# A decoder layer on one core: the first weight loads moved to one queue, in other pieces, with one warming matmul less

## The chip, the cores and the metric

The kernel runs on one core of one Trainium2 chip. The metric is the time of one execution on the device, in microseconds (us). The core has TensorE (PE in the profile; PEld is its weight loader), VectorE (DVE), ScalarE (ACT), GpSimd (POOL) and SyncE (SP). SP and ScalarE can each issue DMA transfers on a queue of their own. Both queues are served by the same 16 DMA engines.

## The reference

One layer of a hybrid decoder on x of 256 tokens and 1024 channels. All data are float32.

```
h = rmsnorm(x, norm1_g)
u = h @ w_in                       # 1024 x 7168: x_rnn, g_rnn, q, k, v, two gates
xa = causal_dwconv(x_rnn)          # width 4
ya = rg_lru(xa) * gelu(g_rnn)
yb = moba_attention(rmsnorm(q), rmsnorm(k), v)
x = x + (sigmoid(g_a) * (ya @ w_proj_rnn) + sigmoid(g_b) * (yb @ w_proj_attn)) @ w_out
h = rmsnorm(x, norm2_g)
x = x + (gelu(causal_dwconv(h @ w_up)) * (h @ w_gate)) @ w_down
```

## The kernel before

**Products in three parts.** Every float32 operand is split into a high part, hi (a copy in the shorter format fp32r), and a remainder, lo = raw - hi. Each product is three matmuls: high by high, high by low, low by high (`mm3`, lines 301 to 304). In the profile L302, L303 and L304 are these three. The hi copy is made on ScalarE (L284, a CAST), the lo subtraction on VectorE (L285).

**The weight stream.** All weights come as a stream of 75 chunks of up to 1 MB (128 partitions by 2048 values), in the order of use. Chunks 0 to 3 are `rx`, the 1024 columns of w_in for the recurrent branch; chunks 4 to 7 are `rg`, its gate; then follow k, the blocks of the recurrent unit, q, v, the two gates, the projections, w_out, and the feed-forward weights. `load_next` issues a chunk's DMA on SP's queue, `split_part` makes its hi and lo, `advance(i)` does both up to chunk i, with loads three chunks ahead. From chunk 4 on, raw, hi and lo tiles rotate in pools of 3, 4 and 3 buffers.

**The order.** TensorE's order follows `UNITS`: rx, rg0 to rg3, k0 and so on. Each unit runs in quarters, and the table `AFTER` says which other work is given out after which quarter: `"rg0.1": "bcast"` gives out the matmul `rbcp` after the second quarter of rg0, `s5` means "split up to chunk 5", `evac0` an evacuation, and so on. A scheduler then puts each engine's instructions in order; an engine executes its queue in that order.

**The norm.** The first product works on x times the gain only (xgh and xgl, the two parts of x^T times `norm1_g`). The row factor 1/rms is applied afterwards: `norm1_stats` squares x in the tiles xs (L397), forms the factor on VectorE (L368 to L374) and two diagonal tiles `dg` (L400). `norm1_bcast` multiplies ones by dg into `rbcp` (L406) and copies it to `rbc` (L407). The evacuations of rx (`rx_evac`, L438) and rg (L680) multiply by rbc.

**The start.** The first four chunks have code of their own (lines 322 to 353 for the loads, 377 to 387 for the splits). Nine matmuls on a tile of ones (L330, `warm`) run first. Then k tiles (pieces of 256 values along each chunk's row: the 128 input channels of one step of the product) are loaded in groups: 0, then 1, then 2 and 3, 4 and 5, 6 and 7. For each group come x^T's part (L344) and one piece of each of the four chunks (L347), 128 KB each for the first two groups and 256 KB after. For k tiles 0 and 1 the pieces of chunks 2 and 3 are issued on ScalarE's queue, all the rest on SP's. `pv` (all small vectors, among them the gain) is the first transfer on ScalarE's queue, and the table load of ScalarE (L349) stands between its DMA issues. The tiles xs are loaded after the pieces of k tiles 4 and 5. `xgh` is made on ScalarE (L382), `xgl` on VectorE (L385). The rx products run k tile by k tile over the four chunks, six matmuls for each pair, 192 in all; for each output the first product needs xgh, hi of the weight piece, then xgl, then lo.

Of the kernel before, what the change touches and what calls it, by code (L numbers as in the profile page):

```python
# [1 line left out]

# [6 lines left out]
F32 = mybir.dt.float32  # L9
F32R = mybir.dt.float32r  # L10
I32 = mybir.dt.int32
AF = mybir.ActivationFunctionType
OP = mybir.AluOpType
AX = mybir.AxisListType

P = 128
S = 256
D = 1024
KT = D // P
# [8 lines left out]
V_CW, V_CB, V_BR, V_BI, V_LAM, V_QG, V_KG, V_G1, V_FW, V_FB, V_G2 = 0, 32, 40, 48, 56, 64, 65, 66, 74, 140, 162  # L28
V_N = 170

HALVES, SMALLS, WARM, RAWS = 22, 10, 9, 3
AHEAD_S, AHEAD_L = 2, 3
DVE_HI = (39, 42, 43)
KEPT = {"ups": 1, "upd": 2, "gts": 1, "gtd": 2, "u": 1, "c": 2, "ah": 3, "al": 3}
# [1 line left out]
         "gb1 gb2 gb3 pr0 pr1 pr2 pr3 pa0 pa1 pa2 pa3")  # L36
AFTER = {
    "rx0.0": "stats s4",
    "rg0.1": "bcast",
    "rg0.2": "s5 evac1",  # L40
    "rg0.3": "s6",
    "rg1.1": "evac0",
    "rg1.3": "evac3 conv0 s7",
    "rg2.0": "evac2",
    "rg2.1": "decay conv1",
    "rg3.0": "split0",
    "rg3.1": "s8",
    "k0.0": "s9",
    "k0.1": "conv2",
    "k0.2": "conv3",  # L50
    "k0.3": "split1",
    "k1.0": "s10",
    "k1.3": "s11",
    "k2.1": "s12",
    "k2.2": "s13",
    "k3.1": "s14 gelu1",
    "ri0.2": "krs",
    "ri0.3": "s15",
    "q0.1": "la0 s16 lb0",
    "q1.1": "s17",  # L60
    "q1.3": "lc0",
    "ri1.0": "s18",
    "q2.0": "ld0",
    "q2.1": "s19",
    "q2.2": "la1",
    "q3.0": "lb1 Tq0",
    "q3.1": "ks0",
    "q3.2": "gelu0",
    "v0.1": "qrs",
    "v0.3": "s20 Tk0",  # L70
    "v1.1": "s21",
    "v2.1": "S0 s22",
    "v3.0": "ks1",
    "v3.1": "Tk1",
    "v3.2": "s23",
    "v3.3": "lc1 S1 S2",
    "ga0.2": "s24 P0",
    "ga1.0": "S3",
    "ga1.1": "s25 P1 O0",
    "ga1.3": "s26",  # L80
    "ga2.0": "Tq1",
    "ga2.1": "P2",
    "ga2.3": "s27",
    "ga3.1": "P3",
    "ga3.2": "O1 S5 S6",
    "ga3.3": "S7 O3",
    "gb0.1": "S4",
    "gb0.3": "s28",
    "gb1.0": "O2",
    "gb1.2": "ld1 s29",  # L90
    "gb1.3": "P4",
    "gb2.0": "s30 s31",
    "gb2.1": "P6 ya0 ya1 O4",
    "gb2.3": "P5",
    "gb3.0": "P7",
    "gb3.1": "ys0",
    "gb3.3": "ys1",
    "pr0.0": "s32 sb0",
    "pr0.2": "sa0",
    "pr0.3": "s33",  # L100
    "pr1.0": "O7",
    "pr1.2": "s34",
    "pr2.0": "sa1 O6",
    "pr2.2": "O5",
    "pr3.3": "sb1",
    "pa0.0": "s35 s36",
    "pa0.3": "s37",
    "pa1.0": "s38",
    "pa2.1": "s39",
    "pa2.2": "s40 m0",  # L110
    "pa3.3": "m1",
    "wo.3": "s41",
    "wo.4": "m2",
    "wo.6": "m3",
    "wo.11": "n10 s42",
    "wo.12": "n00",
    "wo.14": "s43",
    "up00.0": "n01 s44",
    "up00.1": "n11",
    "up00.3": "bcast2",  # L120
    "gt00.0": "s45",
    "up01.0": "s46",
    "gt01.0": "s47",
    "gt01.1": "ur0",
    "up10.1": "s48",
    "up10.2": "gr0",
    "up11.1": "s49",
    "up11.3": "fu0",
    "gt10.1": "s50",
    "gt10.2": "ur1",  # L130
    "gt11.1": "s51 fg0",
    "up20.1": "s52",
    "up20.2": "gr1",
    "up20.3": "fu1",
    "up21.1": "s53",
    "gt20.1": "s54",
    "gt20.2": "ur2",
    "gt20.3": "fg1",
    "gt21.1": "s55",
    "dn0.1": "s56",  # L140
    "dn0.2": "gr2",
    "dn0.3": "fu2",
    "dn1.1": "s57",
    "up30.1": "s58",
    "up30.3": "fg2",
    "up31.1": "s59",
    "gt30.1": "s60",
    "gt30.2": "ur3",
    "gt31.1": "s61",
    "dn2.1": "s62",  # L150
    "dn2.2": "gr3",
    "dn2.3": "fu3",
    "dn3.1": "s63",
    "up40.1": "s64",
    "up40.3": "fg3",
    "up41.1": "s65",
    "gt40.1": "s66",
    "gt40.2": "ur4",
    "gt41.1": "s67",
    "dn4.1": "s68",  # L160
    "dn4.2": "gr4",
    "dn4.3": "fu4",
    "dn5.1": "s69",
    "dn6.1": "s70",
    "dn6.3": "fg4",
    "dn7.1": "s71",
    "last.0": "s72",
    "last.2": "s73",
    "dn8.1": "s74",
}  # L170


# [1 line left out]
def trunk_layer(ctx: ExitStack, tc: tile.TileContext, xT, x, vec, win_fm, win_tm, wri, wpr, wpa,  # L174
# [11 lines left out]
    def half(name, dt=F32):  # L186
        return halfp.tile([P, 1024], dt, tag="half", name=name)
# [4 lines left out]
    def f(ap):  # L192
        return ap.bitcast(F32)
# [4 lines left out]
    class Act:  # L198


        def __init__(self, name, dt=F32):
            self.name, self.dt, self.h = name, dt, {}
# [9 lines left out]
        def pair(self, c):  # L212
            return kt(self.half(c // 2))[:, 2 * (c % 2):2 * (c % 2) + 2, :]

    class Wide:


        def __init__(self, name, dt=F32):
            self.h = [half(f"{name}{i}", dt) for i in range(2)]

        def __getitem__(self, at):
            s = at[1]
            i = s.start // 1024
            assert (s.stop - 1) // 1024 == i
            return self.h[i][:, s.start - i * 1024:s.stop - i * 1024]


    stream = []
# [47 lines left out]
    def split_tiles():  # L276
        i = ptr["split"]
        ptr["split"] += 1
        hi[i] = wp.tile([P, 2048], F32R, tag="hi", name=f"hi{i}", bufs=4)
        lo[i] = wp.tile([P, 2048], F32R, tag="lo", name=f"lo{i}", bufs=3)  # L280
        return i
# [38 lines left out]


    xTs = Act("xT")
    pv = const.tile([P, V_N], F32, name="pv")
    nc.scalar.dma_start(pv, vec)
    ones = const.tile([P, P], F32, name="ones")
    nc.vector.memset(ones, 1.0)
    warm = bank("warm")
# [2 lines left out]
        nc.tensor.matmul(warm[:, :P], ones, ones, start=True, stop=True)  # L330


    pieces = [(0, 1), (1, 2), (2, 4), (4, 6), (6, 8)]
    START = 4
    for i in range(START):
        if i < 2:
            raw[i] = wp.tile([P, 2048], F32, tag="raw", name=f"raw{i}")
            split_tiles()
        else:
            raw[i], hi[i], lo[i] = Wide(f"raw{i}"), Wide(f"hi{i}", F32R), Wide(f"lo{i}", F32R)  # L340
    ptr["load"] = ptr["split"] = START
    xs = const.tile([P, 2, D], F32, name="xs")
    for a, b in pieces:
        nc.sync.dma_start(kt(xTs.half(a // 4))[:, a % 4:a % 4 + b - a, :], xT[:, a:b, :])  # L344
        for i in range(START):
            s = slice(a * 256, b * 256)
            (nc.scalar if b <= 2 and i >= 2 else nc.sync).dma_start(raw[i][:, s], stream[i][:, s])  # L347
        if a == 0:
            nc.scalar.preload_act_table(AF.Exp)  # L349
        if a == 4:  # L350
            for t in range(2):
                nc.sync.dma_start(xs[:, t, :], x[t * P:(t + 1) * P, :])
    load_next(2)

    ident = const.tile([P, P], F32, name="ident")
# [20 lines left out]

    xgh, xgl = Act("xgh", F32R), Act("xgl", F32R)
    with tc.manual_schedule(engines={mybir.EngineType.Activation, mybir.EngineType.DVE}):
        for a, b in pieces:
            for k in range(a, b):  # L380
                g = pv[:, V_G1 + k:V_G1 + k + 1]
                nc.scalar.activation(xgh[k], xTs[k], AF.Copy, scale=g)  # L382
                if a == 0:
                    split_part(0, slice(a * 256, b * 256), True)
                nc.vector.scalar_tensor_tensor(xgl[k], xTs[k], g, f(xgh[k]), op0=OP.mult, op1=OP.subtract)  # L385
            for i in range(a == 0, START):
                split_part(i, slice(a * 256, b * 256))

    rbc = const.tile([P, S], F32, name="rbc")
    rs1 = const.tile([P, 2], F32, name="rs1")  # L390
# [266 lines left out]
    def run_unit(kind, c):  # L657

        i = chunk[kind, c]
        if kind == "rx":  # L660

            for n in range(START):
                rx_ps[n] = kt(psA.tile([P, 512], F32, tag="A", name=f"rx{n}"))
            for k in range(KT):
                for n in range(START):
                    fm_mm(rx_ps[n], n, xgh, xgl, (k,), True)
            yield
            return
        advance(i)
        if kind == "ri":  # L670
            for n4 in range(4):
                ri(c, i, n4)
                yield
        elif kind == "rg":
            ps = fm_ps(f"{kind}{c}")
            for j in range(2):
                for h in range(2):
                    fm_mm(ps, i, xgh, xgl, range(4 * h, 4 * h + 4), js=(j,))
                    if j and h:
                        nc.vector.tensor_mul(gr.pair(c), ps, rbc2)  # L680
                    yield
        else:
            g, kh = c // 2, c % 2
            if not kh:
                open_ps[kind] = [bank(f"pa{g}{t}") if kind == "pa" else
                                 psA.tile([P, 512], F32, tag="A", name=f"{kind}{g}{t}") for t in range(2)]
            ps = open_ps[kind]
            for k4 in range(4):
                tm_mm(ps, i, 4 * kh + k4, k4, *{"pr": (yah, yal), "pa": (ybh, ybl)}.get(kind, (xgh, xgl)),
                      kind not in "qkv")  # L690
                if kh and k4 == 3:
                    evac[kind](g, ps) if kind in evac else qk_evac(kind, g, ps)
                yield
# [19 lines left out]

    def run(name, quarters):
        for q, _ in enumerate(quarters):
            for n in AFTER.get(f"{name}.{q}", "").split():
                advance(int(n[1:])) if n[1:].isdigit() and n[0] == "s" else item[n]()


    yo = {}  # L720
# [289 lines left out]
```

## Time and profile before

| what | value |
|---|---|
| median of three runs | 441.38 us (441.3, 441.38, 441.98) |
| the profiled execution's own time | 442.97 us |
| its span, first to last instruction | 441.2 us |
| TensorE busy | 435.9 us (99%) |
| VectorE busy | 323.9 us (73%) |
| ScalarE busy | 260.6 us (59%) |
| data moved by DMA | 91.68 MB, mean 208 GB/s |

How to read it: a row of the timeline gives the start in us from the span's start, the time in us, engine, line and operation, "out <- in" by the program's names, the shape, and xN for N instructions merged in the row; in square brackets stands how long the engine had been idle before and what ended that. An issue of a DMA stands under SPq or ACTq, with the time that the queue spent issuing, not the transfer's. A row of the windows gives the stretch, its length, the busy time of each engine with its count of instructions, the granted clock of TensorE, the share of the DMA engines and, last, GB/s. A row of the DMA issues gives the queue, the count, the size and the median time in us from issue to landing.

### The profile page before, as it was taken

To read this page: it belongs to the slowest core of one execution; us is meant where nothing else is said; L and a number is where in the kernel's file an instruction comes from. 1 tells how busy PE (TensorE), PEld (TensorE's weight loads), DVE (VectorE), ACT (ScalarE), POOL (GpSimd) and SP (SyncE) were. 2 spreads that over 40 slices of the span, in tenths; PEclk is the share of its full clock that TensorE was granted. 3 is DMA by queue.
4 is the path that set the end of the run, shared out by engine and by line. 5 is a ranking of instruction groups with operands and counts; after the bars stand their busy time and mean duration, and the time that the engine had idled before them with its cause. 6 is when DMAs were issued, how large, how long until landed. Compare 5 with 4: busy or idle time off the path is not lost.

```text
span 441.2 us, 5822 instructions
## 1 busy us (share of the span) xinstructions
PE 435.9 (99%) x2256; PEld 373.2 (85%) x2256; DVE 323.9 (73%) x477; ACT 260.6 (59%) x309; POOL 1.6 (0%) x9
## 2 busy tenths in 40 slices
PE   8999999999999999999999999999999999999996
PEld 8999988887888888888888888888878888888985
DVE  3688995979999775754576796468789775788463
ACT  4686875999996989752322384315737554455420
POOL 1000000000000000000000000000000000000000
PEclk9999999999999999999999999999999999999999
DMA  7996536453584653454553554989579598289302
GB/s 209 386 345 236 191 111 249 173 209 102 187 255 123 192 193 114 171 192 179 194 190 104 192 190 133 318 230 326 174 260 348 193 343 345 90 309 351 110 0 95
DMA packets 27387, 91.68 MB, mean 208 GB/s; under 512 B 2528, under 2 KB 10080, under 8 KB 23264
## 3 DMA queue, kind: packets, MB, share of 16 engines
q1 hardware_dynamic: 26640, 90.71, 60.3%
q10 hardware_dynamic: 720, 0.61, 0.6%
q8 instruction: 17, 0.28, 0.2%
q14 instruction: 10, 0.08, 0.1%
HBM read 85.02 MB, written 6.29 MB: 207 GB/s over the span
## 4 chain that ended last, share of the span: by engine, by line
PE 93%; ACT 5%; DMA 1%; issue 0%; DVE 0%; SPq 0%; ACTq 0%
PE acc L303 4%; PE acc L304 4%; PE acc L302 4%; PE up L304 4%; PE up L302 4%; PE gt L302 4%; PE gt L304 4%; PE gt L303 4%; PE up L303 4%; PE rx L302 2%; PE rx L303 2%; PE rx L304 2%; PE rg L303 2%; PE rg L302 2%; PE rg L304 2%; PE gb L302 2%
## 5 line engine op out<-in xcount | busy, mean ns | idle before, releaser
L285 DVE TENSOR_TENSOR lo<-raw,hi 128x2048 fp32r<-128x2048 f32 (+3 forms) x92 | 170.6, 1866 | 29.6 <-issue 11.4
L284 ACT CAST hi<-raw 128x2048 fp32r<-128x2048 f32 (+3 forms) x88 | 137.5, 1577 | 66.6 <-PE pa L304 16.1
L303 PE MATMUL acc<-lo,fah 128*128 128x512 f32 x80 | 31.2, 391 | 0.0
L303 PE MATMUL gt<-lo,h2h 128*128 128x512 f32 x80 | 31.2, 390 | 0.0
L303 PE MATMUL up<-lo,h2h 128*128 128x512 f32 x80 | 31.2, 390 | 0.0
L304 PE MATMUL up<-hi,h2l 128*128 128x512 f32 x80 | 31.1, 389 | 0.0
L304 PE MATMUL acc<-hi,fal 128*128 128x512 f32 x80 | 31.1, 389 | 0.0
L302 PE MATMUL up<-hi,h2h 128*128 128x512 f32 x80 | 31.1, 390 | 0.0
L304 PE MATMUL gt<-hi,h2l 128*128 128x512 f32 x80 | 31.0, 389 | 0.0
L302 PE MATMUL acc<-hi,fah 128*128 128x512 f32 x80 | 30.6, 389 | 0.0
L302 PE MATMUL gt<-hi,h2h 128*128 128x512 f32 x80 | 30.5, 389 | 0.0
L302 PE MATMUL rx<-xgh,hi 128*128 128x256 f32 x64 | 18.9, 298 | 0.7 <-ACT xgh L382 0.7
L303 PE MATMUL rx<-xgl,hi 128*128 128x256 f32 x64 | 18.8, 293 | 0.0
L304 PE MATMUL rx<-xgh,lo 128*128 128x256 f32 x64 | 18.8, 293 | 0.0
L829 ACT ACTIVATE fc<-fu,pv 128x256 f32<-128x256 f32 x20 | 10.4, 592 | 13.7 <-DVE fu L841 13.7
L302 PE MATMUL rg<-xgh,hi 128*128 128x256 f32 x64 | 18.2, 284 | 0.0
L303 PE MATMUL rg<-xgl,hi 128*128 128x256 f32 x64 | 18.1, 283 | 0.0
L304 PE MATMUL rg<-xgh,lo 128*128 128x256 f32 x64 | 18.1, 283 | 0.0
L303 PEld LDWEIGHTS acc<-lo,fah 128*128 128x128 f32 x80 | 15.0, 188 | 3.5 <-DVE lo L285 0.5
L302 PEld LDWEIGHTS gt<-hi,h2h 128*128 128x128 f32 x80 | 15.0, 188 | 3.2
L304 PEld LDWEIGHTS up<-hi,h2l 128*128 128x128 f32 x80 | 15.0, 188 | 3.1
L304 PEld LDWEIGHTS acc<-hi,fal 128*128 128x128 f32 x80 | 15.0, 188 | 3.1
(247 smaller groups left out, 1061.3 us busy)
## 6 DMA issues: line engine op xcount, KB each, us to landing
raw<-in_win_tm SPq DMA_DIRECT2D x12, 1024.0 KB, 4.8
raw<-in_win_fm SPq DMA_DIRECT2D x11, 1024.0 KB, 5.7
raw<-in_wup SPq DMA_DIRECT2D x11, 1024.0 KB, 6.0
raw<-in_wgate SPq DMA_DIRECT2D x11, 1024.0 KB, 6.5
raw<-in_wdown SPq DMA_DIRECT2D x11, 1024.0 KB, 6.4
raw<-in_wpr SPq DMA_DIRECT2D x4, 1024.0 KB, 4.9
raw<-in_wpa SPq DMA_DIRECT2D x4, 1024.0 KB, 4.9
raw<-in_wout SPq DMA_DIRECT2D x4, 1024.0 KB, 4.8
```

The source lines that it names most:

```text
L284: (nc.vector.tensor_copy if on_dve else nc.scalar.copy)(hi[i][:, s], raw[i][:, s])
L285: nc.vector.tensor_sub(lo[i][:, s], raw[i][:, s], f(hi[i][:, s]))
L302: nc.tensor.matmul(o, ah, bh, start=start, stop=False, skip_group_check=skip)
L303: nc.tensor.matmul(o, ah, bl, start=False, stop=False, skip_group_check=skip)
L304: nc.tensor.matmul(o, al, bh, start=False, stop=stop, skip_group_check=skip)
L829: nc.scalar.activation(c, u, AF.Identity, scale=w(2), bias=pv[:, V_FB + m:V_FB + m + 1])
```

## The change

Beside the table, five things change in the start.

- The warming matmuls are eight (`WARM`).
- ScalarE's queue carries a single transfer, `g1`, the eight columns of the gain (4 KB). `pv` as a whole goes to SP's queue, behind the weights of chunks 0 to 3.
- All weight pieces of chunks 0 to 3 go through SP's queue, in the order of use. For k tile 0 they are one piece of 128 KB for chunk 0, one for chunk 1, and one of 256 KB for chunks 2 and 3; for k tile 1 two of 256 KB; then for each pair of k tiles two of 512 KB, each for two chunks. That is 11 transfers for 20. Behind them come pv, then xs, then chunk 4.
- The splits follow the same pieces: 11 hi copies and 11 lo subtractions. The first hi copy is on VectorE, as before. The tiles for k tiles 0 to 3 are in the rotating pools and those for k tiles 4 to 7 in the pool of half tiles (before: chunks 0 and 1 in the rotating pools, 2 and 3 in half tiles).
- The rx products run k tiles 0, 1, then pairs, in each step over the four chunks. The work given out after rx (the statistics and the split of chunk 4) is held behind the last start split on ScalarE and VectorE (`issue_after`).

The table `AFTER` is written anew in large part. The order of the products on TensorE stays, and so does their number. What stands where on the engines' queues changes; in the built program, VectorE's queue has, after the start, the two halves of chunk 4, the factor's steps, the subtractions of chunks 5 and 6, then dg (before: chunk 4, the factor, dg, then chunks 5 and 6), and the matmul rbcp stands after the third quarter of rg0 (before: the second).

```diff
-HALVES, SMALLS, WARM, RAWS = 22, 10, 9, 3
+HALVES, SMALLS, WARM, RAWS = 22, 10, 8, 3
 AFTER = {
     "rx0.0": "stats s4",
-    "rg0.1": "bcast",
-    "rg0.2": "s5 evac1",
-    "rg0.3": "s6",
-    "rg1.1": "evac0",
-    "rg1.3": "evac3 conv0 s7",
+    "rg0.2": "bcast",
+    "rg1.0": "evac1",
+    "rg1.1": "s5 evac0",
+    "rg1.2": "conv0 conv1",
     "rg2.0": "evac2",
-    "rg2.1": "decay conv1",
+    "rg2.1": "decay",
+    "rg2.2": "s6",
+    "rg2.3": "s7",
...
     "gt20.1": "s54",
-    "gt20.2": "ur2",
-    "gt20.3": "fg1",
-    "gt21.1": "s55",
+    "gt21.0": "ur2 fg1 s55",
...
-    pv = const.tile([P, V_N], F32, name="pv")
-    nc.scalar.dma_start(pv, vec)
+    g1 = const.tile([P, KT], F32, name="g1")
+    nc.scalar.dma_start(g1, vec[:, V_G1:V_G1 + KT])
...
-    for a, b in pieces:
+    def load_x(a, b):
         nc.sync.dma_start(kt(xTs.half(a // 4))[:, a % 4:a % 4 + b - a, :], xT[:, a:b, :])
-        for i in range(START):
-            s = slice(a * 256, b * 256)
-            (nc.scalar if b <= 2 and i >= 2 else nc.sync).dma_start(raw[i][:, s], stream[i][:, s])
-        if a == 0:
-            nc.scalar.preload_act_table(AF.Exp)
-        if a == 4:
-            for t in range(2):
-                nc.sync.dma_start(xs[:, t, :], x[t * P:(t + 1) * P, :])
+
+    def load_w(a, c, js=slice(0, 2), ks=slice(0, 2)):
+        src = win_fm[2 * c + js.start:2 * c + js.stop, :, (2 * a + ks.start) * 256:(2 * a + ks.stop) * 256]
+        nc.sync.dma_start(sraw[a, c][:, js, ks], src.rearrange("c p (k n) -> p c k n", n=256))
+
+    one, two_, both = slice(0, 1), slice(1, 2), slice(0, 2)
+    load_x(0, 1)
+    load_w(0, 0, one, one)
+    nc.scalar.preload_act_table(AF.Exp)
+    load_w(0, 0, two_, one)
+    load_w(0, 1, both, one)
+    load_x(1, 2)
+    for c in range(2):
+        load_w(0, c, both, two_)
+    for a in range(1, 4):
+        load_x(2 * a, 2 * a + 2)
+        for c in range(2):
+            load_w(a, c)
+    pv = const.tile([P, V_N], F32, name="pv")
+    nc.sync.dma_start(pv, vec)
+    for t in range(2):
+        nc.sync.dma_start(xs[:, t, :], x[t * P:(t + 1) * P, :])
     load_next(2)
...
+        def split_x(k):
+            g = g1[:, k:k + 1]
+            nc.scalar.activation(xgh[k], xTs[k], AF.Copy, scale=g)
+            return lambda: nc.vector.scalar_tensor_tensor(xgl[k], xTs[k], g, f(xgh[k]), op0=OP.mult, op1=OP.subtract)
+
+        def split_w(a, c, js=slice(0, 2), ks=slice(0, 2), e=nc.scalar.copy):
+            r, h, l = sraw[a, c][:, js, ks], shi[a, c][:, js, ks], slo[a, c][:, js, ks]
+            start_end[0] = e(h, r).ins
+            return lambda: start_end.__setitem__(1, nc.vector.tensor_sub(l, r, f(h)).ins)
+
+        x = split_x(0)
+        w = split_w(0, 0, one, one, nc.vector.tensor_copy)
+        x()
+        w()
+        split_w(0, 0, two_, one)()
+        split_w(0, 1, both, one)()
+        split_x(1)()
...
-            for k in range(KT):
+            for ks in ((0,), (1,), (2, 3), (4, 5), (6, 7)):
                 for n in range(START):
-                    fm_mm(rx_ps[n], n, xgh, xgl, (k,), True)
+                    fm_mm(rx_ps[n], n, xgh, xgl, ks, True)
...
+            with tc.issue_after(start_end[0]) if name == "rx0" else nullcontext(), \
+                    tc.issue_after(start_end[1]) if name == "rx0" else nullcontext():
```

191 lines of the change are left out of this document (92 added, 99 removed).

## The prediction

> **What bounds the kernel now.** First the page: span, busy time of each engine, chain that ended last.
>
> ```profile
> span 441.2 us, 5822 instructions
> PE 435.9 (99%) x2256; PEld 373.2 (85%) x2256; DVE 323.9 (73%) x477; ACT 260.6 (59%) x309; POOL 1.6 (0%) x9
> PE 93%; ACT 5%; DMA 1%; issue 0%; DVE 0%; SPq 0%; ACTq 0%
> ```
>
> TensorE works through the whole span; only 441.2 - 435.9 = 5.3 us are left, and the change leaves the products as they are (192 rx matmuls before, 192 after). So it can gain in two ways: an earlier first product, or more products at full pace. The timeline of the first 10 us shows both.
>
> ```profile
> 0.74 0.40 ACTq L324 DMA_DIRECT2D pv<-in_vec  x1
> 0.74 0.38 SPq L344 DMA_DIRECT2D xT<-in_xT  x1
> 1.05 4.21 PE L330 MATMUL warm<-ones 128*128 128x128 f32 x18 [1.05 <-DVE ones L326]
> 1.17 0.93 ACTq L347 DMA_DIRECT2D raw<-in_win_fm  x2
> 1.18 0.89 SPq L347 DMA_DIRECT2D raw<-in_win_fm  x2
> 4.36 0.97 ACTq L347 DMA_DIRECT2D raw<-in_win_fm  x2
> 5.00 0.29 DVE L284 CAST hi<-raw 128x256 fp32r<-128x256 f32 x1 [4.00 <-DMA raw<-in_win_fm]
> 5.33 0.43 DVE L285 TENSOR_TENSOR lo<-raw,hi 128x256 fp32r<-128x256 f32 x1
> 5.38 0.51 ACT L382 ACTIVATE xgh<-xT,pv 128x256 fp32r<-128x256 f32 x1 [1.96 <-DMA raw<-in_win_fm]
> 5.79 1.00 ACT L284 CAST hi<-raw 128x256 fp32r<-128x256 f32 x3
> 5.92 0.48 DVE L385 SCALAR_TENSOR_TENSOR xgl<-xT,pv,xgh 128x256 fp32r<-128x256 f32 x1 [0.17 <-ACT xgh L382]
> 5.94 0.88 PE L302 MATMUL rx<-xgh,hi 128*128 128x256 f32 x2 [0.68 <-ACT xgh L382]
> 6.61 0.43 PE L303 MATMUL rx<-xgl,hi 128*128 128x256 f32 x1
> 9.19 0.41 PE L304 MATMUL rx<-xgh,lo 128*128 128x256 f32 x1
> 9.40 0.33 PE L302 MATMUL rx<-xgh,hi 128*128 128x256 f32 x1
> 9.57 0.28 PE L303 MATMUL rx<-xgl,hi 128*128 128x256 f32 x1
> 30.67 0.28 PE L302 MATMUL rg<-xgh,hi 128*128 128x256 f32 x1
> ```
>
> Read it backwards. The first rx product starts at 5.94, on xgh, which ScalarE began only at 5.38, behind its own DMA issues of 4.36 to 5.33. The third product, from which the pace is even, stands at 6.61. It runs at 0.21 us a product until 9.40 (9.19 to 9.40) and at 0.12 afterwards: (30.67 - 9.57) / 175 = 0.12. The profile gives the granted clock as 1.00 throughout, so the step shows in the pace alone.
>
> **The change, part by part.** *Transfers.* Two landings gate the start:
>
> ```profile
> xT<-in_xT SPq DMA_DIRECT2D x1, 128.0 KB, 3.6
> raw<-in_win_fm SPq DMA_DIRECT2D x2, 128.0 KB, 3.9
> 0.00:5.00 5.00, 3.95 (x18) 3.92 (x18) 0.17 (x2) 1.28 (x1) 1.56 (x9) 1.00 0.62 146
> 4.00:5.00 1.00, 1.00 (x6) 0.96 (x5) 0.00 (x1) 0.00 (x0) 0.00 (x0) 1.00 1.07 364
> 5.00:10.00 5.00, 4.32 (x22) 4.06 (x21) 3.94 (x11) 3.04 (x9) 0.00 (x0) 1.00 0.93 241
> 10.00:15.00 5.00, 5.00 (x44) 5.00 (x43) 4.06 (x8) 4.46 (x9) 0.00 (x0) 1.00 1.05 379
> 15.00:20.00 5.00, 5.00 (x44) 5.00 (x44) 2.77 (x5) 1.93 (x4) 0.00 (x0) 1.00 1.02 388
> 20.00:25.00 5.00, 5.00 (x44) 5.00 (x43) 3.47 (x6) 4.22 (x9) 0.00 (x0) 1.00 1.01 367
> 25.00:27.00 2.00, 2.00 (x19) 2.00 (x18) 0.97 (x1) 2.00 (x5) 0.00 (x0) 1.00 1.02 408
> ```
>
> (In the rows of the windows the last column is GB/s.) Before, xT lands at 0.74 + 3.6 = 4.34, the first weight piece at 5.0 (its cast starts then), the second at about 1.63 + 4.0 = 5.6. Until then the ACT queue's transfers, 85 KB of pv and two pieces of 128 KB, share the engines; after, only 4 KB of g1 does. The late bound is that the landings stay. For the early bound, xT loses pv's share, 85 KB at 364 GB/s or 0.23 us: 4.1; the pieces behind it follow at SP's issue pace, 0.89 / 2 = 0.45: 4.55 and 5.0. I take values near the early bound, since the competitor does go: 4.2, 4.6 and 5.05.
>
> *First products.* With no DMA issue in its way, ScalarE makes xgh from 4.25 to 4.76. VectorE casts the first piece from 4.65 to 4.94, so the first product starts at 4.95, after the sixteen warming passes, which end at 1.05 + 4.21 x 16/18 = 4.79: the ninth, which is taken out, would hold it until 5.26. ScalarE casts the second piece from 5.1 to 5.45; the second product starts at 5.55. xgl is done at 5.4, and the third product starts at 5.77 (in the rows above it follows its operand by 0.2: 5.92 + 0.48, then 6.61). That is 6.61 - 5.77 = 0.85 us earlier. Bounds: 0.2, if the second piece's cast still starts at 5.65, and 1.0. The slow pace lasted 9.40 - 5.94 = 3.5 us from the first product. If it lasts as long from 4.95, it ends at 8.4, with 2 + 2.65 / 0.21 = 14.6 slow products for 16: 1.4 x 0.09 = 0.1 more. Start: **0.95 us**.
>
> *Fewer, larger pieces.* Eleven weight DMAs for 20, eleven hi casts and eleven lo subtractions for 20 each: ScalarE and VectorE were idle in part here (3.04 and 3.94 of 5 us), so worth nothing on the path. What TensorE needs in k tiles 2 to 7 lands with the pace of the windows above; two k tiles are 1.31 MB, 3.5 us at 379 GB/s, against 48 products x 0.12 = 5.8 us. Chunk 4, for rg0, is next in SP's queue, now behind 6.4 MB of start, pv and xs; by those windows and the landing delay below it is there at 24.2 and needs at most one 128x2048 cast and subtraction, 1.9 + 2.3: 28.4, for use at 29.7. If that 1.3 us of cover went, rg0 would wait for the difference.
>
> *pv and xs behind all of it.* pv is first read by the convolution at 39.99 (below), 20 us later: free. xs is another matter. It feeds the statistics, these dg, and dg the matmul rbcp that stands among the rg0 products; where instructions stand now decides:
>
> ```profile
> 28.43 1.91 ACT L284 CAST hi<-raw 128x2048 fp32r<-128x2048 f32 x1 [0.44 <-DMA raw<-in_win_fm]
> 30.63 0.48 DVE L400 TENSOR_SCALAR dg<-ident,rs 128x128 f32<-128x128 f32 x2
> 31.03 4.49 DVE L285 TENSOR_TENSOR lo<-raw,hi 128x2048 fp32r<-128x2048 f32 x2
> 31.11 1.91 ACT L284 CAST hi<-raw 128x2048 fp32r<-128x2048 f32 x1 [0.77 <-DVE dg L400]
> 33.55 0.60 PE L406 MATMUL rbcp<-dg,ones 128*128 128x128 f32 x4
> 39.99 2.07 ACT L443 ACTIVATE xa<-xr,pv 128x256 f32<-128x256 f32 x4
> ```
>
> Before, dg ran ahead of the two 128x2048 subtractions (chunks 5 and 6) and was ready at 31.1, 2.4 us before rbcp. After, both subtractions stand ahead of dg in VectorE's queue, and rbcp comes 12 products later (after the third quarter of rg0 for the second). So dg now waits for chunk 6: its DMA, its cast, its subtraction. All of TensorE's work is queued behind rbcp, and ScalarE's copy of it with the evacuations behind that.
> Bytes up to the end of chunk 6: 5.24 MB (start), 0.09 (pv), 1.05 (xs), 3 x 1.05 (chunks 4 to 6): 9.53. Moved by 5 us, as before: 0.73 MB. To 10 us at 364 instead of 241 GB/s, since the queue no longer runs empty: 2.55. To 25 us at 379, 388 and 367: 8.22. The last 1.31 at 408: end at 28.2. Landing: chunk 5's cast began at 28.43, and the 8.48 MB up to it were through at 27.15 by the same windows, 1.3 us earlier. So chunk 6 lands at 29.5; bounds 28.6 (0.4 MB more moved by 10 us) and 31.0 (as before: its cast began at 31.11). Cast to 31.45, subtraction (4.49 / 2) to 33.75, first half of dg to 34.0, rbcp 34.1: 4.6 after the landing. TensorE is there at 30.67 + 36 x 0.12 = 34.99, less 0.95: 34.05. A wait of 0.1 us.
>
> *Later order.* The hand-written table moves splits in many places. One shows what that is worth:
>
> ```profile
> 314.58 4.49 DVE L285 TENSOR_TENSOR lo<-raw,hi 128x2048 fp32r<-128x2048 f32 x2
> 322.55 0.39 PE L303 MATMUL acc<-lo,fah 128*128 128x512 f32 x1
> 323.16 3.45 DVE L832 SCALAR_TENSOR_TENSOR fc<-fu,pv,fc 128x255 f32<-128x255 f32 x8
> PEld acc L303 <- DVE lo L285: 0.5, 1, 0.5
> ```
>
> The first wdown chunk's subtraction ended at 319.1, 3.5 us ahead of its use at 322.55; now eight convolution steps (3.45) go ahead of it: cover about gone, cost 0 to 0.2. The next chunk's subtraction, which made TensorE's loader wait 0.5, moves ahead of 1.29 us of other work: gain 0.2 to 0.5. Together nothing.
>
> *Sum.* 0.95 - 0.1 gives 0.8 us (rounded down, as that wait can only grow): span 440.4, profiled execution 442.97 - 0.8 = 442.2 (1.8 lie outside the span). The median, 441.38, is 1.6 under the profiled execution; the same 0.8 off gives **440.6**.
>
> **Rivals.** The end is the earlier of two gains: the start's, and 34.99 - (landing of chunk 6 + 4.6).
> *Early clock step:* warming and rx are now nearly joined (4.79, then 4.95), where a hole of 0.68 lay before; if the step comes near 6, some 11 slow products become 0.09 faster each: 1.0 more, 1.95 in all. The statistics cap it: 0.9 with the landing at 29.5, 1.8 at 28.6; halfway gives 1.4. For it: the small hole. Against: 4.21 us of unbroken warming did not bring the step. Time 440.0 (439.4 to 440.4).
> By the Trainium skill (TensorE: Matmul & The Clock Gate, "What's actually happening") a busy window of about 3.4 us raises the clock and the windows run free of the kernel. The 3.5 us above agrees. By that rule the step's place is chance, and sixteen passes (3.74 us) hold a whole window less often than eighteen (4.21): (0.8 - 0.33) / 3.4 = 14% less often, times the 1.4 us that 16 slow products cost: an estimate of 0.2 us against the change. With it the sum would be 440.8.
> *Statistics late (slower):* chunk 6 lands at 31.0 as before; rbcp waits until 35.6; 0.6 slower, 442.0. It decides from a landing of 30.4 on. For it: 1 MB of xs went behind. Against: DMA idled in 5 to 10 us before.
> *Start not earlier (the reordered queue brings nothing):* the landings stay and ScalarE's freedom alone gives 0.2: 441.2. For it: xT, with 128 KB and the first place, still took 3.6, so most of that is delay and not bytes. Against: the landings, 4.34, 5.0 and 5.6, are 0.6 apart, more than SP's 0.45.
> *A later split misses its product (slower):* one subtraction comes late by its own length, 2.3, net 1.5: 442.9. For it: the cover of the first wdown chunk is gone. Against: over all splits before, the loader waited once for one, 0.5.
> *Later waits vanish:* the wait above and a like one go: 0.5 more: 440.1.
>
> **How the numbers follow.** Forecast 39%, early step 24%, statistics late 12%, no earlier start 9%, split missed 9%, waits vanish 7%. The time is the forecast's, 440.6; its own range 440.0 to 441.1. For 8 in 10: 439.4 to 442.1, which leaves out the tail of the first rival and the missed split. 0.2% is 0.9 us, about what a measurement tells from no change. Below 440.5: 13 of the 39, 23 of 24, 6 of 7: 42%. Above 442.3: 3 of 12, 8 of 9: 11%. The rest 47%.
>
> **What would show it.** First rx product at 4.8 to 5.2, third at 5.8; pace to 0.12 near 8.4 (or 6); chunk 6's cast near 29.5, ahead of dg; rbcp at 34.1 with TensorE waiting on dg 0 to 0.5 us; the wdown chunk's loader wait gone. Wrong if the first rx product is past 5.7, if rbcp waits over 1 us, or if TensorE waits over 0.5 us anywhere after 40.

## The result, and the profile after

The changed kernel is slower: median 443.14 us (442.42 to 444.3, 20 runs) against 442.05 (441.3 to 443.27, 20 runs), ratio 1.0024 with the interval 1.0015 to 1.0032. That is 1.1 us lost where 0.8 was forecast as gained. (The forecast of 440.6 was counted from 441.38, the median of three runs of before; with twenty that median is 442.05, so 0.7 of the distance from 440.6 to 443.14 is the base alone.) The profiled execution took 442.78 us with a span of 441.0; the one of before, 442.97, lay 0.9 above its median, so this pair by itself does not show the loss. First the page of after: span, busy time, the chain that ended last, and two groups of rx products with the idle time before them.

```profile
span 441.0 us, 5783 instructions
PE 434.4 (98%) x2254; PEld 371.5 (84%) x2254; DVE 323.5 (73%) x468; ACT 258.4 (59%) x299; POOL 1.5 (0%) x9
PE 91%; DMA 5%; issue 1%; DVE 1%; ACT 1%; SPq 0%
L292 PE MATMUL rx<-xgh,his 128*128 128x256 f32 x64 | 18.3, 288 | 1.1 <-ACT his L400 1.1
L294 PE MATMUL rx<-xgh,los 128*128 128x256 f32 x64 | 18.3, 286 | 1.0 <-DVE los L401 1.0
```

DMA now holds 5% of the chain where it held 1%, and 2.1 us of idle time stand ahead of rx products. The timeline of after shows where:

```profile
3.30 0.51 ACT L395 ACTIVATE xgh<-xT,g 128x256 fp32r<-128x256 f32 x1 [0.84 <-DMA g<-in_vec]
4.49 0.55 PE L292 MATMUL rx<-xgh,his 128*128 128x256 f32 x2
4.87 0.28 PE L293 MATMUL rx<-xgl,his 128*128 128x256 f32 x1
4.99 0.28 PE L294 MATMUL rx<-xgh,los 128*128 128x256 f32 x1
5.94 0.28 PE L294 MATMUL rx<-xgh,los 128*128 128x256 f32 x1
6.39 0.62 ACT L400 CAST his<-raws 128x512 fp32r<-128x512 f32 x1 [1.81 <-DMA raws<-in_win_fm]
7.07 0.39 PE L292 MATMUL rx<-xgh,his 128*128 128x256 f32 x1 [0.84 <-ACT his L400]
7.79 0.39 PE L294 MATMUL rx<-xgh,los 128*128 128x256 f32 x1 [0.23 <-DVE los L401]
11.29 1.05 ACT L400 CAST his<-raws 128x1024 fp32r<-128x1024 f32 x1 [0.41 <-DMA raws<-in_win_fm]
12.37 2.58 DVE L401 TENSOR_TENSOR los<-raws,his 128x1024 fp32r<-128x1024 f32 x2 [0.98 <-ACT his L400]
12.39 0.39 PE L292 MATMUL rx<-xgh,his 128*128 128x256 f32 x1 [0.28 <-ACT his L400]
13.65 0.39 PE L294 MATMUL rx<-xgh,los 128*128 128x256 f32 x1 [0.76 <-DVE los L401]
```

The start is earlier than forecast: third product at 4.87 (6.61 before, forecast 5.77), and the pace is 0.12 us from there on (4.87, 4.99), so the step that came at 9.40 before is past already. Both gains are then lost in four stretches without a product ("holes" from here on): 0.84 and 0.23 us on the 256 KB piece of chunks 2 and 3, which is cast only at 6.39, and 0.28 and 0.76 on the first 512 KB piece, cast at 11.29 in one step of 1.05 us and subtracted in one of 1.3. Counted from one product's start to the next, against the pace of 0.12, the four cost 2.7 us, and the first product after each takes 0.1 more: 3.1 in all. The third place is rbcp, where the rows of after stand as the prediction described them, 1 us later:

```profile
30.52 1.91 ACT L274 CAST hi<-raw 128x2048 fp32r<-128x2048 f32 x1 [0.42 <-DMA raw<-in_win_fm]
32.79 2.29 DVE L275 TENSOR_TENSOR lo<-raw,hi 128x2048 fp32r<-128x2048 f32 x1
34.99 0.48 DVE L429 TENSOR_SCALAR dg<-ident,rs 128x128 f32<-128x128 f32 x2
35.33 0.71 PE L435 MATMUL rbcp<-dg,ones 128*128 128x128 f32 x4
```

Chunk 6 lands at 30.4 to 30.5 (forecast 29.5), and rbcp starts 4.9 us after it. TensorE was there at about 35.1 and its loader waited 0.3. The waits of TensorE's loader over the whole span, after and then before, show the third effect: with the new table two waits of 0.5 are gone, against a new one of 0.4.

```profile
PEld rx L292 <- ACT his L400: 1.5, 2, 1.0
PEld rx L294 <- DVE los L401: 1.4, 2, 1.0
PEld warm L320 <- DVE ones L316: 1.1, 1, 1.1
PEld yo L294 <- DVE ml L289: 0.4, 2, 0.2
PEld pt L620 <- DVE kTl L578: 0.4, 1, 0.4
...
PEld rbcp L435 <- DVE dg L429: 0.3, 1, 0.3
```

```profile
PEld rx L302 <- ACT xgh L382: 1.0, 1, 1.0
PEld Tq L546 <- ACT it L463: 0.5, 1, 0.5
PEld acc L303 <- DVE lo L285: 0.5, 1, 0.5
```

**A ruler for all runs.** Behind rbcp hardly anything varies: span less start of rbcp is 441.0 - 35.33 = 405.7 here and 405.5 to 405.8 in every experiment with the new table. With the old table it is 441.2 - 33.55 = 407.6, less twelve products of 0.12 that stand before rbcp in the new order, 406.2; and the same, 440.1 - 32.46 - 1.4 = 406.2, in the second profile with it. So the later order is worth about 0.5 us, and each profile is told by the start of rbcp. With the 1.8 us of an execution that lie outside the span, the median of after puts rbcp at 443.14 - 1.8 - 405.7 = 35.6, that of before, counted in the new order, at 442.05 - 1.8 - 406.2 = 34.05: the first 35 us lose 1.6, the rest gives 0.5 back.

### The profile page after: what moved, and what is told of

Read it like the earlier page. It is cut to its first block, busy times and chain, and to the rows that moved or that the text cites. A ratio compares the mean times of both kernels' runs of the same rounds, so it can differ in the third digit from the quotient of the medians.

```text
span 441.0 us, 5783 instructions
## 1 busy us (share of the span) xinstructions
PE 434.4 (98%) x2254; PEld 371.5 (84%) x2254; DVE 323.5 (73%) x468; ACT 258.4 (59%) x299; POOL 1.5 (0%) x9
## 4 chain that ended last, share of the span: by engine, by line
PE 91%; DMA 5%; issue 1%; DVE 1%; ACT 1%; SPq 0%
PE acc L292 4%; PE acc L293 4%; PE acc L294 4%; PE gt L293 4%; PE up L293 4%; PE up L292 4%; PE gt L292 4%; PE gt L294 4%; PE up L294 4%; DMA raws<-in_win_fm 3%; DMA raw<-in_win_fm 2%; PE gb L292 2%; PE yo L294 2%; PE ga L292 2%; PE pr L292 2%; PE pa L292 2%
## 5 line engine op out<-in xcount | busy, mean ns | idle before, releaser
L275 DVE TENSOR_TENSOR lo<-raw,hi 128x2048 fp32r<-128x2048 f32 (+1 forms) x72 | 160.1, 2225 | 44.1 <-ACT hi L274 9.2
L274 ACT CAST hi<-raw 128x2048 fp32r<-128x2048 f32 (+1 forms) x69 | 128.1, 1862 | 69.0 <-PE pa L294 13.0
L292 PE MATMUL rx<-xgh,his 128*128 128x256 f32 x64 | 18.3, 288 | 1.1 <-ACT his L400 1.1
L294 PE MATMUL rx<-xgh,los 128*128 128x256 f32 x64 | 18.3, 286 | 1.0 <-DVE los L401 1.0
L293 PE MATMUL rx<-xgl,his 128*128 128x256 f32 x64 | 18.0, 282 | 0.0
L294 PEld LDWEIGHTS gt<-hi,h2l 128*128 128x128 f32 x80 | 15.0, 188 | 3.1
```

The lines of the kernel that those rows point to most:

```text
L274: (nc.vector.tensor_copy if on_dve else nc.scalar.copy)(hi[i][:, s], raw[i][:, s])
L275: nc.vector.tensor_sub(lo[i][:, s], raw[i][:, s], f(hi[i][:, s]))
L292: nc.tensor.matmul(o, ah, bh, start=start, stop=False, skip_group_check=skip)
L293: nc.tensor.matmul(o, ah, bl, start=False, stop=False, skip_group_check=skip)
L294: nc.tensor.matmul(o, al, bh, start=False, stop=stop, skip_group_check=skip)
```

## The experiments

All were timed in five rounds beside the kernel before; where an interval holds 1, no difference to it is shown, and where two intervals overlap, none between the two is. The last two columns are from the profile of one execution each; in e14, which has the old table, rbcp stands twelve products earlier.

| run | median us (runs) | ratio to before, interval | rbcp starts | span |
|---|---|---|---|---|
| changed kernel | 443.14 (20) | 1.0024, 1.0015 to 1.0032 | 35.33 | 441.0 |
| e1 pieces per chunk | 444.79 (6) | 1.0061, 1.0042 to 1.0081 | 36.86 | 442.5 |
| e2 steps halved | 443.64 (12) | 1.0037, 1.0018 to 1.0056 | 36.63 | 442.3 |
| e3 before, new table | 441.65 (12) | 0.9989, 0.9975 to 1.0003 | 34.21 | 439.8 |
| e4 nine warming | 443.50 (12) | 1.0036, 1.0022 to 1.0050 | 38.00 | 443.6 |
| e5 dg first | 442.88 (12) | 1.0023, 1.0007 to 1.0039 | 36.51 | 442.1 |
| e6 ScalarE's queue | 442.24 (12) | 0.9998, 0.9984 to 1.0011 | 34.44 | 440.2 |
| e7 = e5 + e6 | 441.94 (12) | 0.9984, 0.9969 to 0.9998 | 34.15 | 439.7 |
| e8 = e2 + e5 | 441.77 (12) | 0.9984, 0.9967 to 1.0000 | 34.49 | 440.1 |
| e9 = e2 + e5 + e6 | 442.12 (12) | 0.9979, 0.9962 to 0.9997 | 34.73 | 440.3 |
| e10 one piece there | 442.09 (12) | 0.9991, 0.9978 to 1.0004 | 34.85 | 440.5 |
| e11 = e3, one queue | 442.60 (12) | 1.0010, 0.9990 to 1.0029 | 35.62 | 441.3 |
| e12 = e9, k tile by k tile | 441.59 (12) | 0.9976, 0.9960 to 0.9993 | 33.18 | 439.0 |
| e13 = e12, eleven warming | 440.71 (12) | 0.9970, 0.9955 to 0.9984 | 33.14 | 438.7 |
| e14 before, twelve warming | 441.81 (12) | 1.0005, 0.9990 to 1.0021 | 32.46 | 440.1 |
| e15 = e12, one queue | 440.97 (12) | 0.9978, 0.9966 to 0.9990 | 33.86 | 439.4 |

**Three theories: pieces, table, clock.** Theory A: the coarse pieces make the holes. B: the later order costs the time. C: eight warming matmuls do.

*Pieces per chunk (e1).*

```
-    load_w(0, 1, both, one)
+    for j in (one, two_):
+        load_w(0, 1, j, one)
...
         for c in range(2):
-            load_w(a, c)
+            for j in (one, two_):
+                load_w(a, c, j)
```

> The changed kernel with each weight piece of the start that holds two chunks cut into one for each chunk (256 KB becomes 128, 512 becomes 256), and cast and subtracted chunk by chunk; queue, order, table and warming stay. Theory A (coarse pieces: TensorE's holes among the rx products, 0.84 us behind the 256 KB piece and 0.28 and 0.76 us behind the first 512 KB piece, are what the change lost): about 1 us faster than the changed kernel, 442.0 (441.5 to 442.5), the holes that end on 128x1024 halved. Theory B (the later order in the table costs it) and theory C (eight warming matmuls for nine raise the clock later): as the changed kernel, 443.1 (442.8 to 443.5).

444.79: all three missed. Cutting by chunk does not help. In this profile the whole queue is slower, as the windows show (last column GB/s), first of after, then of e1; the four other profiles with the DMAs of after (e2, e4, e5, e8) have 251 to 293 in this stretch:

```profile
5.00:10.00 5.00, 3.93 (x31) 3.52 (x30) 2.50 (x5) 2.30 (x5) 0.00 (x0) 1.00 0.94 283
```

```profile
5.00:10.00 5.00, 5.00 (x40) 5.00 (x39) 2.46 (x8) 2.67 (x7) 0.00 (x0) 1.00 0.86 224
```

The rx products end no later than in after (the last starts at 30.56, there at 30.66). The loss is made at rbcp: chunk 6 is cast at 32.04 (30.52 in after), and rbcp, at 36.86, came 2.0 behind the product before it. That wait, which no theory had, was the lead to theory D.

*Steps halved (e2): DMAs as in the change, casts and subtractions chunk by chunk.*

```
-                split_w(a, c)()
+                for j in (one, two_):
+                    split_w(a, c, j)()
```

> The changed kernel with its DMAs as they are, but each cast and subtraction of a two-chunk piece in two steps, one for each chunk. Theory A, if the grain of the casts matters: the hole before the first los of k tiles 2 and 3 falls from 0.76 to about 0.1 us and the one before his from 0.28 to 0; 0.8 us faster, 442.3. Theory A, if the landing of the pieces matters: 0.3 us or less, 442.8 to 443.1. Theories B and C: 443.1.

443.64, no gain, though the step had worked in part: in the profile the hole before the first los fell from 0.76 to 0.23 and the last product ahead of rbcp started 0.5 us earlier than in after (34.43 against 34.98). (The hole before his grew from 0.28 to 0.94: TensorE came there earlier, and the first product of the 512 KB piece still started at 12.38.) Then it stood. The rows of VectorE and TensorE in e2:

```profile
34.09 2.28 DVE L275 TENSOR_TENSOR lo<-raw,hi 128x2048 fp32r<-128x2048 f32 x1
36.30 0.47 DVE L432 TENSOR_SCALAR dg<-ident,rs 128x128 f32<-128x128 f32 x2
36.63 0.71 PE L438 MATMUL rbcp<-dg,ones 128*128 128x128 f32 x4 [1.92 <-DVE dg L432]
```

dg stands behind the subtraction of chunk 6 and TensorE idles 1.92 us for it. The gain was made and lost again 20 us later.

*The kernel before with the new table (e3).*

```
-    "rg0.1": "bcast",
+    "rg0.2": "bcast",
...
```

> The kernel before with the changed kernel's table of due times and nothing else: its start, queues, pieces and nine warming matmuls stay. Theory B: slower than before by about 1 us, 443.0 (442.6 to 443.5). Theories A and C: 0 to 0.4 us faster than before, 441.6 to 442.1, since the statistics are early here and the two small stalls of before, 0.24 and 0.2 us, go.

441.65: B falls, as no loss of 1 us is there. By the ruler the new order is good for half a us; the interval agrees, but holds 1.

*Nine warming matmuls (e4).*

```
-HALVES, SMALLS, WARM, RAWS = 22, 10, 8, 3
+HALVES, SMALLS, WARM, RAWS = 22, 10, 9, 3
```

> The changed kernel with nine warming matmuls, as before. Theory C: half of the loss or more comes back, 442.0 to 442.6, and in most profiles the products are at 0.12 us from the first. Theories A and B: 443.1 (442.8 to 443.5); the first product may start 0.2 us later, behind the ninth, which the holes take up.

443.50: C falls. Its profile, the slowest of all, has another thing to show. Holes of 0.85, 0.22, 0.73 and 0.76 us stood among the products from 9.8 to 15.1, and then the granted clock fell (third column from the end):

```profile
12.00:14.00 2.00, 1.27 (x11) 1.07 (x10) 1.03 (x3) 1.34 (x2) 0.00 (x0) 1.00 1.05 400
15.84:19.26 3.42, 3.42 (x18) 3.42 (x17) 3.27 (x5) 2.94 (x5) 0.00 (x0) 0.50 1.07 391
```

For 3.42 us TensorE ran at half clock, 1.7 us lost, on top of the holes themselves. None of the other profiles has this, but it was not a single case. That execution's granted clock is 0.995, and 14 of the 194 executions of the changed kernel and the experiments stand at 0.995 or 0.996, all others at 0.998 or more. The 14 are all of kernels with one queue: 1 of 20 of the changed kernel, 2 of 6 in e1, and of twelve each 2 in e2, 3 in e4, 4 in e5 and 2 in e11. (Of the many runs of before timed beside them, one stands at 0.996.)

**Theory D: rbcp waits for chunk 6.** *dg ahead of the two subtractions (e5).*

```
+        with tc.issue_after(dg_done[-1]) if i in (5, 6) else nullcontext():
             nc.vector.tensor_sub(lo[i][:, s], raw[i][:, s], f(hi[i][:, s]))
```

> The changed kernel with the two dg ahead of the subtractions of chunks 5 and 6 in VectorE's order, as they stood before; nothing else. Theory D (new; the statistics cost it: dg stands behind the subtraction of chunk 6, so rbcp starts no earlier than 4.9 us after chunk 6 lands, however early TensorE is; it waited 0.35, 2.0 and 2.2 us in three of four profiles with this start): dg ends near 31, rbcp starts without a wait at 34.4 to 35 us, and the median falls by about 1.2 to 441.9 (441.4 to 442.5). Theory A (holes among the rx products): 0.35 us at most, 442.7 to 443.2.

The mechanism is as expected, the size is not: 442.88, 0.3 and not 1.2. In the profile of e5 (443.91 us, 1.0 above its median) dg ends at 32.0 and rbcp does not wait, but TensorE itself is late, with holes of 1.09 and 0.76 us on the first 512 KB piece. Without the four executions at the lower clock the median is 442.65, which is still not 441.9:

```profile
31.56 0.48 DVE L432 TENSOR_SCALAR dg<-ident,rs 128x128 f32<-128x128 f32 x2
31.96 4.49 DVE L276 TENSOR_TENSOR lo<-raw,hi 128x2048 fp32r<-128x2048 f32 x2
36.51 0.61 PE L438 MATMUL rbcp<-dg,ones 128*128 128x128 f32 x4
```

So there are two limits of about the same height: the holes (A) and chunk 6 (D), and rbcp starts at the later of the two. Taking away one leaves the other. *Steps halved and dg first (e8)* is the test, since neither showed a gain alone:

> dg first, with the casts and subtractions of two-chunk pieces in two steps (DMAs as in the changed kernel). Theory D with A: the smaller steps are worth 0.5 to 0.8 us once rbcp doesn't hold TensorE: 441.2 (440.8 to 441.7). Theory D alone: 441.9.

441.77, 1.4 below the changed kernel, where e2 gave -0.5 and e5 0.3. The interval of e8 touches none of the three: dg in its old place is worth 0.9984 against 1.0037 once the steps are halved, and halved steps 0.9984 against 1.0023 once dg is first. No execution of e8 has the lower clock; against the other eight of e5 (442.65) its gain is 0.9. In its profile rbcp follows the last product without a wait, and the holes on the first 512 KB piece are 0.77 and 0.23:

```profile
12.31 0.39 PE L295 MATMUL rx<-xgh,his 128*128 128x256 f32 x1 [0.77 <-ACT his L403]
13.04 0.39 PE L297 MATMUL rx<-xgh,los 128*128 128x256 f32 x1 [0.23 <-DVE los L404]
34.49 0.61 PE L441 MATMUL rbcp<-dg,ones 128*128 128x128 f32 x4
```

*The two 256 KB pieces of chunks 2 and 3 on ScalarE's queue (e6), and with dg first (e7).*

```
+    load_w(0, 1, both, one, nc.scalar)
+    load_w(0, 1, both, two_, nc.scalar)
     nc.scalar.preload_act_table(AF.Exp)
     load_w(0, 0, two_, one)
-    load_w(0, 1, both, one)
```

> The changed kernel with the two 256 KB pieces of chunks 2 and 3 (k tiles 0 and 1) on ScalarE's queue, issued ahead of its table load; dg stays last. Theory A (one queue brings the second piece late): it lands by 5.2 us instead of 5.6 to 6.4, the first hole goes, 442.2 to 442.6. Theory D: whatever the start gains, rbcp still waits for chunk 6, 442.9 to 443.4, and TensorE only waits longer there.

> The edits of the two runs above together. Theory D with A: the start's gain comes through now that rbcp doesn't hold it: 441.3 (440.8 to 441.8), faster than with dg first alone by 0.5. Theory D alone, if the queue brings nothing: 441.9.

442.24 and 441.94. The interval of e6 does not touch that of the changed kernel, nor that of e7 that of e5: with the large pieces the second queue is worth 0.9 us. Both limits moved: chunk 6's cast starts at 29.62 in e6 (30.52 in after), so even with dg last rbcp starts at 34.44, after a wait of 0.5 (its loader's 0.7). What the second queue does shows in the stretch from 4 to 6 us; the rows of after, e6, e11 and e3, in this order (last column GB/s):

```profile
4.00:6.00 2.00, 2.00 (x16) 2.00 (x15) 1.05 (x3) 0.41 (x1) 0.00 (x0) 1.00 0.92 187
```

```profile
4.00:6.00 2.00, 1.46 (x6) 0.99 (x6) 1.24 (x4) 1.16 (x3) 0.00 (x0) 1.00 1.07 356
```

```profile
4.00:6.00 2.00, 2.00 (x11) 2.00 (x11) 1.30 (x4) 0.49 (x3) 0.00 (x0) 1.00 0.86 246
```

```profile
4.00:6.00 2.00, 1.75 (x9) 1.35 (x9) 1.52 (x4) 1.28 (x4) 0.00 (x0) 1.00 0.97 306
```

**Theory Q: the slow packets at 4 to 6 us come with the single queue.** *Three edits (e9), and with only the piece of k tile 0 on ScalarE's queue (e10).* e9 puts the edits of e2, e5 and e6 together; e10 takes `load_w(0, 1, both, two_)` back to SyncE's queue.

> The changed kernel with three edits: dg ahead of the subtractions of chunks 5 and 6, the two 256 KB pieces of chunks 2 and 3 on ScalarE's queue, and casts and subtractions of two-chunk pieces in two steps. Theory D with A: 441.2 (440.8 to 441.7), rbcp without a wait at 33.5 to 34.2 us; what follows rbcp takes 402.2 us as in every profile with the later table. If the steps bring nothing beside the queue: 441.9, as with the first two edits.

> The three edits, but of the two pieces only that of k tile 0 on ScalarE's queue; that of k tile 1 is back on SyncE's. Theory Q (the slow packets, over 0.3 us each, that hold up the third piece at 4 to 5 us come with a single queue): the first dip goes, 0.8 MB moved by 5 us instead of 0.70, but the one at 7 to 9 us stays; 441.5 (441.1 to 442.0). If only the issue order on SyncE's queue counts: as the three edits, 441.2.

Both miss their times. (The 402.2 us that the expectation of e9 puts behind rbcp are not the ruler's 405.6.) Theory Q's sign in the rate came: e10 moves 347 GB/s from 4 to 6 us. The twelve runs of e9 fall into two groups, 440.56 to 440.89 (five) and 442.12 to 442.66 (seven); those of e10 lie all between 441.90 and 442.30. The pace of 0.21 us lasts until 9.43 in the profile of e9 (442.12 us) and until 9.78 in that of e10 (442.26); in that of e12 (440.76, below) it is 0.12 from 6.06 on. By these three profiles the kernels are quick or slow by where the step of the clock falls, about 1.5 us apart, and so e10 does not tell how much the one piece does.

*The kernel before with the new table and one queue (e11).*

```
-            (nc.scalar if b <= 2 and i >= 2 else nc.sync).dma_start(raw[i][:, s], stream[i][:, s])
+            nc.sync.dma_start(raw[i][:, s], stream[i][:, s])
```

> The kernel before with the later table, and with all weight pieces of the start on SyncE's queue in the old order and size (pv stays on ScalarE's). Theory Q: the pieces of chunks 2 and 3 for k tile 0 land after 5.5 us, TensorE gets a hole there, 1 us slower than with two queues, 442.6 (442.2 to 443.2). If the one queue does no harm and the changed kernel's loss is in its pieces alone: 441.7.

442.60, 0.95 over e3, as theory Q had it, though the two intervals overlap; the rows above show the rate. The place was another: the hole, 1.56 us, came at 13.4, behind k tile 1.

*k tiles 2 and 3 one after the other, in four pieces of 256 KB (e12).*

```
+        if a == 1:
+            for c in range(4):
+                load_w(a, c % 2, both, (one, two_)[c // 2])
+            continue
...
-            for ks in ((0,), (1,), (2, 3), (4, 5), (6, 7)):
+            for ks in ((0,), (1,), (2,), (3,), (4, 5), (6, 7)):
```

> The three edits, with k tiles 2 and 3 loaded, split and multiplied one k tile after the other (256 KB pieces) as k tiles 0 and 1 are. Theory A: the hole of 0.7 to 1.4 us that all profiles of this start show at 11 to 13 us, ahead of the first 512 KB piece, falls to 0.5 or less: 440.6 (440.2 to 441.2). If the bytes before it set it, whatever the piece: 441.2.

The profile has no hole at 11 to 13 us, as A said, but that of e9 has none either. The time again has two groups, six runs from 440.52 to 441.04 and six from 442.14 to 442.44. Group by group that is e9 again (medians 440.6 and 440.6, 442.2 and 442.4), so with two queues and halved steps the smaller pieces gained nothing that shows. Theory G: the hole that the second queue leaves between warming and the third product (0.68 us idle in e12, whose step came early all the same) can let the step slip. *Eleven warming matmuls close it (e13); twelve close that of the kernel before (e14).* Only `WARM` changes.

> The kernel that goes k tile by k tile (three edits on top), with eleven warming matmuls for eight, so that TensorE has no hole between warming (to about 5.8 us) and the third rx product (6.06). Theory G (the step of the clock comes at the end of an unbroken busy stretch of some 3.4 us; a hole behind the warming puts it off to 9.4 to 9.8, which costs 1.5 us): all runs in one group near 440.8, none of those near 442.3; median 440.8 (440.5 to 441.1). If the two groups of six runs have another cause: two groups again, median 441.6.

> The kernel before with twelve warming matmuls for nine, which end near 6.2 us, where its third rx product stands at 6.61. Theory G: the step comes by 7.9 at the latest, runs of 442.3 and more go, median 441.5 (441.2 to 441.8). Then what the changed kernel loses at an equal clock is 1.6 us and not 1.1, for its products follow the warming without a hole already. If the step's place is worth nothing: 442.0 to 442.2, the two products that start later adding 0 to 0.2.

e13: one group, 440.37 to 441.33, median 440.71. G stands there, and this is the lowest median of all, 0.3% under the kernel before (interval 0.16 to 0.45%). The first rows of its timeline:

```profile
1.05 4.91 PE L323 MATMUL warm<-ones 128*128 128x128 f32 x22 [1.05 <-DVE ones L319]
5.72 0.48 PE L295 MATMUL rx<-xgh,his 128*128 128x256 f32 x2
6.04 0.28 PE L296 MATMUL rx<-xgl,his 128*128 128x256 f32 x1
6.16 0.28 PE L297 MATMUL rx<-xgh,los 128*128 128x256 f32 x1
```

e14 does not follow: 441.81, no change that the interval shows, and two of its twelve runs lie over 443. The late step is at most a small part of the median of before. So the loss at an equal clock stays near 1.1 us, and what spreads the runs of before is open. The 17 profiles together speak for G, as a matter of chance: in the ten without a hole ahead of the third product the pace is 0.12 by 7.5 us at the latest; of the seven with one, of 0.18 to 0.68 us, three (before, e9, e10) keep 0.21 until 9.4 to 9.8, the other four do not.

*One queue again (e15): e12 with all weight pieces on SyncE's queue.*

> The kernel that goes k tile by k tile, with eight warming matmuls and all weight pieces of the start on SyncE's queue again. Theory Q: 4 to 6 us at about 200 GB/s instead of 367, holes of 1 us or more behind the second piece or k tile 1, 442.4 (441.9 to 443.0). If the smaller pieces of k tiles 2 and 3 make the second queue needless: 441.6.

440.97, with ten of twelve runs from 440.75 to 441.21: theory Q as put there falls in the time. The one queue is still slow from 4 to 6 us and leaves a hole:

```profile
4.00:6.00 2.00, 2.00 (x14) 1.92 (x14) 1.14 (x3) 0.41 (x1) 0.00 (x0) 1.00 0.88 208
7.63 0.39 PE L295 MATMUL rx<-xgh,his 128*128 128x256 f32 x1 [1.14 <-ACT his L407]
10.38 1.37 ACT L407 CAST his<-raws 128x512 fp32r<-128x512 f32 x2 [0.20 <-DMA raws<-in_win_fm]
```

But the 1.14 us are the only hole left among the products, and these follow the warming without one, so no second group stands apart. Against e13, whose runs are one group too, the queue costs 0.26 us, with overlapping intervals: behind small pieces its cost is not shown. With one queue throughout, three edits lead from the changed kernel to 2.2 us less: 443.14, dg first 442.88, halved steps 441.77, k tiles 2 and 3 one by one 440.97. Of these the second is clear of noise, and so are the first two together; the third is 0.8 by the medians but 0.0006 (0.3 us) by the ratios, whose intervals overlap, and shows in the profiles (rbcp at 33.86 against 34.49).

## Why the prediction was wrong

The step that failed is "Fewer, larger pieces": "What TensorE needs in k tiles 2 to 7 lands with the pace of the windows above", and so "worth nothing on the path". It compared the rate of a pair of k tiles (3.5 us) with its products (5.8 us), which holds once the stream runs, and left out the first piece of each kind: it has to land whole, and then be cast and subtracted whole, before its first product. For k tiles 2 and 3 that is a cast at 11.29, 1.05 and 1.3 us of steps, and two holes; for chunks 2 and 3 of k tile 0 it is a cast at 6.39, behind a transfer that landed late, and two more. What stood at nothing cost 3.1 us in the profile. e8 shows it: with halved steps on the same queue, and dg first, the time comes back. The second queue brings most of it back too (e6, e7), with the large steps, so the late landing belongs to the cause; e15 points to the size of the pieces, without being clear of noise.

Profile against profile the sum closes. The start gains 1.7 (6.61 to 4.87) and the early step 1.3 (some fourteen products at 0.21 in place of 0.12); the holes take 3.1 and rbcp 0.2, and the later order gives 0.5 back: 0.2 faster, as the spans say. The medians have it 1.1 slower, since the profile of before lies 0.9 above its median and that of after 0.4 below its own.

Point by point:

- *The bytes.* "To 10 us at 364 instead of 241 GB/s, since the queue no longer runs empty: 2.55" failed as well: after has 283 GB/s from 5 to 10 us, and 2.1 MB. It misread its own row: the DMA share there is 0.93 before (0.94 after), so the engines had hardly been idle, the packets were slow; the rival's "DMA idled in 5 to 10 us before" rests on the same misreading. With two pieces on ScalarE's queue e6 moved 336 GB/s there, and 2.52 MB by 10 us.
- *The start.* Right in sign, too small: third product 1.7 us earlier, forecast 0.85. The early bound for xT took only pv's bytes as the competitor; what else delayed xT before was not found. Part of the 1.7 lies in the profile of before itself: the third product of the same start stands at 5.90 in e3.
- *The clock.* The rival "early clock step" came true in the profile (0.12 from 4.87 on, forecast 8.4). The reason named, the joined warming and rx, fits the 17 profiles above, as a better chance and not as a rule. Its gain and the start's went into the holes: rx took 24.6 us before (5.94 to 30.55) and 26.2 after (4.49 to 30.66). Weighing sixteen passes against eighteen by the Trainium skill (TensorE: Matmul & The Clock Gate, "What's actually happening") gave 0.2 us against the change. No run here bears that out: e4, with eighteen, was no faster.
- *The statistics.* Mechanism and place were right, rbcp bound to chunk 6 plus 4.9 (forecast 4.6). The wait was mis-sized, 0.1 forecast, 0.3 in the profile of after and 1.92 in e2; the rival decided from a landing of 30.4 on, and the landing was 30.4. Its rbcp of 35.6 is where the ruler puts the median of after. But it is not the whole cause: with dg first (e5) all but 0.3 us of the loss stayed.
- *The later order.* Forecast as nothing, worth about 0.5; "later waits vanish" came true, and hid a third of the 1.6 us that the first 35 lose.
- *What would show it wrong.* Of the three signs none came: first rx product at 4.49, rbcp waiting 0.3, nothing over 0.5 after 40 us. The list had no sign for a hole between 6 and 14 us, the very place that the argument had set to nothing.

## What to carry to other kernels

At the start of a stream, follow the first piece of each size by itself: when its last byte lands, then its cast and subtraction as whole steps, then its first product; a rate over several pieces says nothing about that. Where two limits end on the same matmul (here the holes and dg behind chunk 6), an edit on one alone shows little or nothing, so try them together before a theory is dropped. And take a fixed point behind the change, like rbcp here, from which all profiles take the same time: it turns each of them into one number.

## What the runs showed of the hardware

- With all weight pieces on SyncE's queue the DMA engines moved 178 to 246 GB/s from 4 to 6 us in all eight profiles (187 in after), with the early pieces spread over two queues 306 to 367 in nine, e3 and before among them. Three pairs differ in the queue alone: e11 and e3 (246 and 306), e8 and e9 (203 and 366), e15 and e12 (208 and 367). The Trainium skill (DMA: Bandwidth & Descriptors, "Issuing engines are not separate DMA queues") says that a second issuing engine saves only the issue time; these 2 us go against it, as the engines were busy 86 to 94% of them with one queue too. By 10 us less of it is left, 1.8 to 2.1 MB moved against 1.9 to 2.5: before and e3, with two queues, have their slow spell later (from 6 to 10 us 233 and then 217 GB/s in before, 178 and then 237 in e3). Single packets of 1 KB, 0.05 us in the median, took up to 1.35 in the first 10 us (up to 0.87 with two queues). Why was not found.
- A DMA is as late as the slowest of its 16 engines: the 256 KB piece of chunks 2 and 3 in after reached half of its engines' ends by 4.65 us and the last at 6.37. For the transfers behind it the distance was 0.7 to 0.9 us until 18 us and 1.5 from 20 to 30. It is not a matter of one queue: before has 0.1 to 0.5 until 16 us and 0.8 to 1.4 from there.
- Holes can cost twice: in e4 2.6 us of them within 5.5 us were followed by 3.42 us at half clock. The Trainium skill (TensorE: Matmul & The Clock Gate, "What's actually happening") has a busy window of about 3.4 us that raises the clock, and an idle one that lowers it. The length agrees, while the stretch before the fall was not idle: of the emptiest 3.4 us TensorE was busy 56%. The profiles of e1, e5 and e11 have 3.4 us with only 46 to 48% busy and no fall, though other executions of these three stand at 0.995 or 0.996. These four kernels have 11 of the 14 executions at the lower clock, in 42 of the 194; so few busy microseconds go with the fall here, and do not decide it.
